# Expert outputs through DRAM rows for seven expert pairs instead of five, written by index, and one more weight buffer

## The chip, the cores and the metric

One core of a Trainium2 chip runs the whole kernel. The metric is the device time of one execution in microseconds (us): the median of the runs shown.

## The reference, cut to what matters

One decoder layer on 512 tokens of 1024 numbers: two attention branches, then a mixture of 32 experts, of which every token takes two, and a final RMSNorm. The change lies in the mixture:

```python
expert_id = g_sel[:, None] * EXPERTS_PER_GROUP + top_idx      # two experts of one group for each token
weight = p_group * jax.nn.softmax(top_vals, axis=-1)
...
def expert_block(args):
    xb, e = args
    return (jax.nn.silu(xb @ w_g[e]) * (xb @ w_u[e])) @ w_d[e]   # 1024 -> 256 -> 1024
...
out = jnp.zeros((T, D), h.dtype).at[slot_tok].add(ys * slot_w[:, None])
```

Every expert has three weight matrices of 1 MB in float32 (gate, up, down), 96 MB for all 32.

## The kernel before

The work runs in this order: RMSNorm and transposes; the projections and the attention of the first branch (MLA), then of the second (MoBA); the merge gates; the product with w_out, with the router's arithmetic between its matmuls; then the experts, two at a time, in 16 steps q = 0 to 15 (`experts`, L862); then the final norm.

**Slots.** Each expert has 64 slots, a pair fills 128 partitions: the first 64 are one expert's, the others the next one's. The 512 tokens take two experts each, so 1024 of the 2048 slots hold a token; in an empty slot the token number `xf` is 0 (tokens are counted from -1024, L663 and L1234), and its row index `xi` is 1024, outside the table. A path for experts with more than 64 tokens (`overflow`, L993) exists; in this execution it does nothing.

**One step.** TensorE multiplies the pair's rows `xT` with the gate weights (32 matmuls, L778), then with the up weights (32, L778); ScalarE and VectorE make the activation `a`; TensorE transposes it (L790) and multiplies with the down weights (16, L804). The rows of pair q + 2 are fetched by index from DRAM on the POOL queue (`gather_rows`, L731: rows `xg`, router weights `wg`) during step q, and transposed in step q + 1 (L755).

**Two ways for a pair's output to reach the tokens.** Pairs that are not in `VIA = (1, 3, 5, 7, 9)` are combined: the output is split into a high and a low part (L811, L812), a one-hot matrix `S` of slots by tokens is made (L817), and for each of 8 pieces (2 halves of the columns, 4 token tiles) two matmuls (L824, L825) bring the rows to their tokens and one VectorE addition (L826) adds them to `x2`. These 8 pieces are done in the next step or the next two: from step 1 to step 10 at most four in a step (L899), after that all eight. The five pairs in `VIA` write the output, 128 rows of 4 KB with the empty slots, to the DRAM table `yd` by one plain DMA of POOL (`down_out`, L843). In steps 10 to 13, two indirect DMAs of POOL a step (`take_slots`, L852) fetch for the 128 tokens of one tile the row of each choice, where that choice lies in a `VIA` pair; two VectorE additions (L914) add them in the step after.

**Weights.** SP's queue loads the weights of the experts, one DMA of 1 MB for each matrix (`load`, L686); each waits until the third last one has landed (L688), so at most three are in flight, and until its buffer is free. `new_w` (L677) deals out NH = 20 buffers of 8 KB a partition in a ring: buffer 0 has a place of its own, the others are spaces that the attention and the w_out stage leave. The output tile `y` has another space, 2 x 4 KB a partition (tag "yd", L846 and L855). The loads of a pair come as gate, gate, up, up, down, down.

**Order.** PE and POOL in the expert stage run in the order in which the code is written (L869); elsewhere a scheduler orders the instructions of a queue. Each queue runs in order: an instruction that waits holds up all behind it.

Of the kernel before, what the change touches and what calls it, by code (L numbers as in the profile page):

```python
# [10 lines left out]
F32 = mybir.dt.float32  # L11
# [3 lines left out]
I32 = mybir.dt.int32  # L15
# [6 lines left out]
P = 128  # L22
# [10 lines left out]
NH = 20  # L33
VIA = (1, 3, 5, 7, 9)


class Layer:
# [310 lines left out]
    def moba_qkv(self):  # L348
# [5 lines left out]
        self.V[1] = self.half("Vb", F32, (NT, 512))  # L354
        late = []

        def split_T(which, t, qr):
# [32 lines left out]
    def attention(self, br, pairs):  # L390
# [4 lines left out]
        for m in pairs:  # L395
# [30 lines left out]
            for i, k in ((i, k) for i in range(NT) for k in range(i + 1)):  # L426
                for h in range(2):
                    hh = 2 * m + h
                    E = Es[2 * i + h][2]
                    mm = nc.tensor.matmul(O[64 * h:64 * h + 64, i * P:(i + 1) * P], self.V[br][:, k, hh * 64:(hh + 1) * 64],  # L430
                                          E[:, k * P:(k + 1) * P], start=k == 0, stop=k == i)
                    if first is None:
                        first = mm
                        for c in PT[2:]:
                            self.after(mm, c)
# [198 lines left out]
    def route_setup(self):  # L634
# [8 lines left out]
        for g in range(4):  # L643
# [13 lines left out]
                          .to_broadcast([P, 32]))  # L657
        self.rc = c.tile([P, 33 + NT + NE], F32, name="rc")
        self.load_late(self.rc, io["rconst"])
        self.iota32 = self.rc[:, 0:32]  # L660
        self.slot = self.rc[:, 32:33]
        self.token = self.rc[:, 33:33 + NT]
        self.base = self.rc[:, 33 + NT:]  # L663
        self.tri = c.tile([P, 2, P], F16, name="tri")
# [12 lines left out]
    def new_w(self):  # L677
        i = self.nw % NH
        self.nw += 1
        if i == 0:  # L680
            return self.bl.tile([P, 2048], F32, name="w", tag="w", bufs=1)
# [146 lines left out]
    def slot_rows(self):  # L828
# [11 lines left out]
        self.yi = c.tile([P, NT, 2], I32, name="yi")  # L840
        nc.vector.tensor_tensor(self.yi, rows, far, ALU.add)

    def down_out(self, wd, aT, sw, q):  # L843

        nc = self.nc
        y = self.bl.tile([P, D], F32, name="y", tag="yd", bufs=2)  # L846
        for h in range(2):
            nc.scalar.mul(y[:, h * 512:h * 512 + 512], self.down_products(wd, aT, h), sw)
        i = VIA.index(q) * P
        nc.gpsimd.dma_start(self.yd[i:i + P], y)  # L850

    def take_slots(self, t, i):  # L852

        nc = self.nc
        y = self.bl.tile([P, D], F32, name="y", tag="yd", bufs=2)  # L855
        nc.gpsimd.memset(y, 0.0)
# [5 lines left out]
    def experts(self):  # L862
# [6 lines left out]
        with tc.manual_schedule(engines={mybir.EngineType.PE, mybir.EngineType.Pool}):  # L869
            xT, sw, xg = {0: self.xT0}, {}, {}  # L870
            S, y, todo, taken = None, None, [], []
            for q in range(NP):
# [11 lines left out]
                def between(j):  # L884
                    if q == 0 and j == 3:
                        self.tokens()
                        xg[1] = self.gather_rows(self.xi[:, 1:2], self.rows)
                    if q == 0 and j == 5:
                        sw[0] = self.take_weights()
# [7 lines left out]
                if q == 0:  # L897
                    next_rows()
                n = min(len(todo), 4) if VIA[0] <= q <= VIA[-1] + 1 else len(todo)  # L899
                some((n + 1) // 2 + (n > 4))  # L900
                aT = self.act_T(*a)
                if q:
                    sw[q] = [self.slot_weights(q, wg, nc.scalar.copy)[:, 0:1]]
                some(n // 2 - (n > 4))
                if 0 < q < NP - 1:
# [145 lines left out]
    def run(self):  # L1051
        tc, ctx = self.tc, self.ctx
        self.oT = [None, None]
        self.nw, self.loads, self.rf = 0, [], {}
        PS = dict(space=PSUM, reuse_waits="tile")
# [157 lines left out]
def shape_consts():  # L1213
# [15 lines left out]
    out["tri"] = tri  # L1229
    rc = np.zeros((P, 33 + NT + NE), np.float32)  # L1230
    rc[:, 0:32] = np.arange(32)
    rc[:, 32] = 1025 + np.arange(P) % 64
    rc[:, 33 + NT:] = [64 * (2 * VIA.index(i // 2) + i % 2) - 1025 if i // 2 in VIA else 1 << 20 for i in range(NE)]
    rc[:, 33:33 + NT] = np.arange(P)[:, None] + P * np.arange(NT)[None, :] - 1024  # L1234
    out["rconst"] = rc
    out["tm"] = np.broadcast_to(np.arange(T, dtype=np.float32) - 1024, (P, T)).copy()
# [31 lines left out]
```

## Time and profile before

| | |
|---|---|
| median of 3 runs | 682.37 us (682.04 to 683.69) |
| the profiled execution | 683.7 us |
| its span, first to last instruction | 681.9 us |
| mean granted TensorE clock | 0.989 of full speed |
| TensorE busy with matmuls | 661.3 us (97%) |
| VectorE, ScalarE, POOL busy | 376.1, 283.3, 83.3 us |
| moved by DMA | 152.06 MB, mean 223 GB/s |

The profiled execution is the slowest of the three; 1.8 us of it lie outside its span, and it is 1.3 us above the median. Matmuls are pipelined, so that a busy TensorE is one that has been given work, not one at its peak. Idle time of an engine that is not the bound costs nothing.

### The profile page before, as it was taken

The page shows a single profiled execution, that of the slowest core. Times are in us where ns is not written, and L with a number is a line of the kernel's source. Part 1 is how long each engine was busy: PE and PEld are TensorE (multiplying, and loading weights), DVE is VectorE, ACT ScalarE, POOL GpSimd, SP SyncE. Part 2 cuts the span into 40 slices and gives each one's busy share as a digit, 9 for nine tenths or more (in the row PEclk, how much of TensorE's full clock was granted, in tenths as well). Part 3 has the DMA queues.
Part 4 walks back from the last instruction along what each step waited for, and adds up shares of the span by engine and source line. Part 5 has one row for each costly group of instructions (what it writes and reads, how often), then busy time and mean ns, then how long its engine had stood idle before and what let it go on. Part 6 is the DMA issues. An engine that isn't in the chain of part 4 may idle for free.

```text
span 681.9 us, 11080 instructions
## 1 busy us (share of the span) xinstructions
PE 661.3 (97%) x4182; PEld 508.6 (75%) x4182; DVE 376.1 (55%) x944; ACT 283.3 (42%) x653; POOL 83.3 (12%) x127
## 2 busy tenths in 40 slices
PE   7999999999999999999999999999999999999991
PEld 7998887777788888888888899755666566666651
DVE  4624957877847983533568224643234332566654
ACT  4737545654639673433334153322222222222223
POOL 0604000000000000000000001212111111334303
PEclk8999999999999999999999999999999999999996
DMA  7733442101073026221398948799999999999953
GB/s 254 128 103 66 86 163 73 62 1 62 15 200 96 1 63 185 68 87 62 137 331 306 392 169 287 256 408 408 409 415 416 410 410 414 415 412 416 413 194 125
DMA packets 75656, 152.06 MB, mean 223 GB/s; under 512 B 31860, under 2 KB 54476, under 8 KB 63824
## 3 DMA queue, kind: packets, MB, share of 16 engines
q1 hardware_dynamic: 67616, 138.70, 55.9%
q0 software_dynamic: 4944, 8.35, 3.6%
q10 hardware_dynamic: 3040, 4.27, 2.4%
q8 instruction: 34, 0.56, 0.3%
q14 instruction: 22, 0.18, 0.1%
HBM read 149.57 MB, written 6.88 MB: 229 GB/s over the span
## 4 chain that ended last, share of the span: by engine, by line
PE 92%; DVE 4%; ACT 1%; DMA 1%; issue 1%; POOL 0%; SPq 0%; POOLq 0%; DVEq 0%
PE yp L804 8%; PE G L778 8%; PE U L778 8%; PE pacc L97 5%; PE pacc L96 5%; PE pacc L95 5%; PE pacc L451 4%; PE pacc L449 4%; PE pacc L450 4%; PE cp L824 3%; PE ptr L422 3%; PE cp L825 3%; PE S L404 3%; PE O L430 2%; PE pacc L493 2%; PE pacc L494 2%
## 5 line engine op out<-in xcount | busy, mean ns | idle before, releaser
L66 DVE SCALAR_TENSOR_TENSOR wlo<-wraw,ms,whi 128x256 fp32r<-128x256 f32 (+2 forms) x134 | 68.3, 551 | 31.1 <-ACT whi L65 30.9
L65 ACT ACTIVATE whi<-wraw,ms 128x256 fp32r<-128x256 f32 (+2 forms) x134 | 67.0, 560 | 42.1 <-PE pacc L450 19.8
L95 PE MATMUL pacc<-whi,hThi 128*128 128x352 f32 (+1 forms) x192 | 73.0, 380 | 0.0
L96 PE MATMUL pacc<-wlo,hThi 128*128 128x352 f32 (+1 forms) x192 | 70.4, 368 | 0.0
L97 PE MATMUL pacc<-whi,hTlo 128*128 128x352 f32 (+1 forms) x192 | 70.4, 366 | 0.0
L784 DVE SCALAR_TENSOR_TENSOR a<-U,wg,a 128x256 f32<-128x256 f32 x15 | 10.3, 686 | 101.8 <-issue 68.9
L804 PE MATMUL yp<-w,a 128*64 128x512 f32 x256 | 58.5, 598 | 0.5 <-ACT a L792 0.5
L778 PE MATMUL G<-w,xT 128*64 128x256 f32 x512 | 58.3, 380 | 0.0
L778 PE MATMUL U<-w,xT 128*64 128x256 f32 x512 | 58.2, 379 | 0.0
L778 PEld LDWEIGHTS G<-w,xT 128*64 128x64 f32 x512 | 36.5, 137 | 24.6 <-issue 4.9
L826 DVE TENSOR_TENSOR x<-x,cp 128x512 f32<-128x512 f32 x88 | 54.2, 682 | 0.8 <-PE cp L825 0.8
L778 PEld LDWEIGHTS U<-w,xT 128*64 128x64 f32 x512 | 36.7, 137 | 18.4
L449 PE MATMUL pacc<-hThi,whi 128*128 128x512 f32 x128 | 50.4, 393 | 0.0
L451 PE MATMUL pacc<-hThi,wlo 128*128 128x512 f32 x128 | 50.3, 393 | 0.0
L450 PE MATMUL pacc<-hTlo,whi 128*128 128x512 f32 x128 | 49.9, 390 | 0.0
L417 ACT ACTIVATE E<-E,mx 128x128 f32<-128x128 f32 (+3 forms) x64 | 35.6, 558 | 20.4 <-DVE mx L414 19.6
L1107 POOL TENSOR_SCALAR sq<-sq 128x1 f32<-128x1 f32 x4 | 0.9, 220 | 343.4 <-ACT junk L1104 343.4
L95 PEld LDWEIGHTS pacc<-whi,hThi 128*128 128x128 f32 x192 | 36.5, 190 | 4.9 <-issue 1.4
L96 PEld LDWEIGHTS pacc<-wlo,hThi 128*128 128x128 f32 x192 | 36.6, 191 | 4.2 <-issue 0.7
L804 PEld LDWEIGHTS yp<-w,a 128*64 128x64 f32 x256 | 17.0, 136 | 30.2 <-issue 27.8
L97 PEld LDWEIGHTS pacc<-whi,hTlo 128*128 128x128 f32 x192 | 36.4, 189 | 3.9 <-issue 0.2
L824 PE MATMUL cp<-yhl,S 128*128 128x512 f32 x88 | 37.6, 427 | 0.0
(232 smaller groups left out, 1338.8 us busy)
## 6 DMA issues: line engine op xcount, KB each, us to landing
w<-in_w_exp_gate_dram SPq DMA_DIRECT2D x32, 1024.0 KB
w<-in_w_exp_up_dram SPq DMA_DIRECT2D x32, 1024.0 KB
w<-in_w_exp_down_dram SPq DMA_DIRECT2D x30, 1024.0 KB
wraw<-in_w_in_dram SPq DMA_DIRECT2D x14, 1024.0 KB
wraw<-in_w_out_dram SPq DMA_DIRECT2D x4, 1024.0 KB
wraw<-in_w_in_dram SPq DMA_DIRECT2D x5, 704.0 KB
yd<-y POOLq DMA_DIRECT2D x5, 512.0 KB, 8.5
xs<-in_x_dram SPq DMA_DIRECT2D x4, 512.0 KB
```

The costliest lines, as they stand in the source:

```text
L65: nc.scalar.mul(hi[:, k], raw[:, k], g)
L66: nc.vector.scalar_tensor_tensor(lo[:, k], raw[:, k], g, hi[:, k].bitcast(F32), ALU.mult, ALU.subtract)
L95: nc.tensor.matmul(ps[t][:, :ncols], act_hi[kk // 4][:, kk % 4, ts], hi[:, k], start=kk == 0, stop=False)
L96: nc.tensor.matmul(ps[t][:, :ncols], act_hi[kk // 4][:, kk % 4, ts], lo[:, k], start=False, stop=False)
L97: nc.tensor.matmul(ps[t][:, :ncols], act_lo[kk // 4][:, kk % 4, ts], hi[:, k], start=False, stop=kk == ktot - 1)
L449: nc.tensor.matmul(ps, hi[:, k, ds], self.hT[0][k // 4][:, k % 4], start=k == 0, stop=False)
L450: nc.tensor.matmul(ps, hi[:, k, ds], self.hT[1][k // 4][:, k % 4], start=False, stop=False)
L451: nc.tensor.matmul(ps, lo[:, k, ds], self.hT[0][k // 4][:, k % 4], start=False, stop=k == KD - 1)
L778: nc.tensor.matmul(GU[i][es, 0:256], xT[:, j, es], gu[e][i][:, j * 256:(j + 1) * 256], start=j == 0, stop=j == KD - 1)
L804: nc.tensor.matmul(yp[es], aT[:, j, es], wd[e][:, j * D + half * 512:j * D + half * 512 + 512], start=j == 0, stop=j == 1)
L824: nc.tensor.matmul(cp, S[:, t * P:(t + 1) * P], y[0], start=True, stop=False)
L826: nc.vector.tensor_tensor(self.x2[t][:, hs], self.x2[t][:, hs], cp, ALU.add)
```

## The change

The pairs that go through DRAM become (1, 2, 4, 5, 7, 8, 9). Their rows are written by an indirect DMA whose index `yw` sends empty slots out of bounds, where nothing is written. So that every row of `yd` has been written once, two DMAs of SP copy 512 and 384 rows of `x` into it, after the first matmul of the first attention that multiplies with V (L430). The eight pieces of a combined pair are spread evenly over the steps up to the next combined pair: (3, 3, 2) over three steps, (2, 2, 2, 2) over four, eight in one step after pair 10 and later. The two halves of `y` become one tile of 8 KB a partition, `yy`, which first serves as a weight buffer for the very first load; the ring of 20 begins with the second. The router weights of pair 0 are taken (L888) after the eighth group of gate matmuls instead of the sixth.

```diff
--- before.py
+++ after.py
@@ -31,7 +31,7 @@
 NEG = -1e30
 NE = 32
 NH = 20
-VIA = (1, 3, 5, 7, 9)
+VIA = (1, 2, 4, 5, 7, 8, 9)
 
 
 class Layer:
@@ -353,6 +353,9 @@
         self.KB = [self.ktiles(n, F32R) for n in ("KBhi", "KBlo")]
         self.V[1] = self.half("Vb", F32, (NT, 512))
         late = []
+        for i in range(0, len(VIA) * P, T):
+            n = min(T, len(VIA) * P - i)
+            self.after(nc.sync.dma_start(self.yd[i:i + n], self.io["x"][0, 0:n, :]), self.first_pv)
 
         def split_T(which, t, qr):
             qf = qr.rearrange("p h c -> p (h c)")
@@ -431,6 +434,8 @@
                                           E[:, k * P:(k + 1) * P], start=k == 0, stop=k == i)
                     if first is None:
                         first = mm
+                        if (br, m) == (0, 0):
+                            self.first_pv = mm
                         for c in PT[2:]:
                             self.after(mm, c)
             self.evac_split(self.oT[br][0][:, m], self.oT[br][1][:, m], O)
@@ -655,12 +660,13 @@
         self.load_late(self.rb[:, 0:4], io["b_router_group"][0:1, :].to_broadcast([P, 4]))
         self.load_late(self.rb[:, 8:40], io["b_router_expert"].rearrange("o g e -> o (g e)")
                           .to_broadcast([P, 32]))
-        self.rc = c.tile([P, 33 + NT + NE], F32, name="rc")
+        self.rc = c.tile([P, 33 + NT + NE + len(VIA)], F32, name="rc")
         self.load_late(self.rc, io["rconst"])
         self.iota32 = self.rc[:, 0:32]
         self.slot = self.rc[:, 32:33]
         self.token = self.rc[:, 33:33 + NT]
-        self.base = self.rc[:, 33 + NT:]
+        self.base = self.rc[:, 33 + NT:33 + NT + NE]
+        self.own = self.rc[:, 33 + NT + NE:]
         self.tri = c.tile([P, 2, P], F16, name="tri")
         self.after(nc.gpsimd.dma_start(self.tri, io["tri"]), self.started)
         self.tm = c.tile([P, T], F16, name="tm")
@@ -675,8 +681,11 @@
 
 
     def new_w(self):
-        i = self.nw % NH
+        i = (self.nw - 1) % NH
         self.nw += 1
+        if self.nw == 1:
+            self.yy = self.bl.tile([P, 2048], F32, name="w", tag="yd", bufs=1)
+            return self.yy
         if i == 0:
             return self.bl.tile([P, 2048], F32, name="w", tag="w", bufs=1)
         pool, tag = {11: (self.wp, "wraw"), 12: (self.wp, "wraw"), 13: (self.wp, "whi"), 14: (self.wp, "wlo"),
@@ -839,20 +848,30 @@
         nc.vector.tensor_tensor(rows, rows, self.place, ALU.add)
         self.yi = c.tile([P, NT, 2], I32, name="yi")
         nc.vector.tensor_tensor(self.yi, rows, far, ALU.add)
+        free = c.tile([P, NE // 2], F32, name="free")
+        nc.vector.tensor_scalar(free, self.xf, -0.5, float(1 << 20), ALU.is_gt, ALU.mult)
+        self.yw = c.tile([P, len(VIA)], I32, name="yw")
+        for i, q in enumerate(VIA):
+            nc.vector.tensor_tensor(self.yw[:, i:i + 1], free[:, q:q + 1], self.own[:, i:i + 1], ALU.add)
+
+    def new_y(self):
+        self.ny += 1
+        return self.yy[:, self.ny % 2 * D:self.ny % 2 * D + D]
 
     def down_out(self, wd, aT, sw, q):
 
         nc = self.nc
-        y = self.bl.tile([P, D], F32, name="y", tag="yd", bufs=2)
+        y = self.new_y()
         for h in range(2):
             nc.scalar.mul(y[:, h * 512:h * 512 + 512], self.down_products(wd, aT, h), sw)
-        i = VIA.index(q) * P
-        nc.gpsimd.dma_start(self.yd[i:i + P], y)
+        i = VIA.index(q)
+        nc.gpsimd.indirect_dma_start(out=self.yd, out_offset=bass.IndirectOffsetOnAxis(ap=self.yw[:, i:i + 1], axis=0),
+                                     in_=y, in_offset=None, bounds_check=len(VIA) * P - 1, oob_is_err=False)
 
     def take_slots(self, t, i):
 
         nc = self.nc
-        y = self.bl.tile([P, D], F32, name="y", tag="yd", bufs=2)
+        y = self.new_y()
         nc.gpsimd.memset(y, 0.0)
         nc.gpsimd.indirect_dma_start(out=y, out_offset=None, in_=self.yd,
                                      in_offset=bass.IndirectOffsetOnAxis(ap=self.yi[:, t, i:i + 1], axis=0),
@@ -885,7 +904,7 @@
                     if q == 0 and j == 3:
                         self.tokens()
                         xg[1] = self.gather_rows(self.xi[:, 1:2], self.rows)
-                    if q == 0 and j == 5:
+                    if q == 0 and j == KD - 1:
                         sw[0] = self.take_weights()
                     if q == 0 and j == 9:
                         self.count_blocks()
@@ -896,12 +915,13 @@
                         self.gathered_T(xg[q + 1][0], xT[q + 1], g)
                 if q == 0:
                     next_rows()
-                n = min(len(todo), 4) if VIA[0] <= q <= VIA[-1] + 1 else len(todo)
-                some((n + 1) // 2 + (n > 4))
+                n = -(-len(todo) // next(d for d in range(1, NP) if q + d - 1 not in VIA))
+                first = n if n < 4 else (n + 1) // 2 + (n > 4)
+                some(first)
                 aT = self.act_T(*a)
                 if q:
                     sw[q] = [self.slot_weights(q, wg, nc.scalar.copy)[:, 0:1]]
-                some(n // 2 - (n > 4))
+                some(n - first)
                 if 0 < q < NP - 1:
                     next_rows()
                 if q + 1 < NP:
@@ -1051,7 +1071,7 @@
     def run(self):
         tc, ctx = self.tc, self.ctx
         self.oT = [None, None]
-        self.nw, self.loads, self.rf = 0, [], {}
+        self.nw, self.ny, self.loads, self.rf = 0, 0, [], {}
         PS = dict(space=PSUM, reuse_waits="tile")
         SB = dict(reuse_waits="tile")
         ctx.enter_context(tc.tile_pool(name="edge", bufs=1, side="right")).tile([P, 24], F32, name="pad")
@@ -1227,11 +1247,12 @@
     tri[:, 0] = np.arange(P)[:, None] <= np.arange(P)[None, :]
     tri[:, 0] += 1024.0 * np.eye(P)
     out["tri"] = tri
-    rc = np.zeros((P, 33 + NT + NE), np.float32)
+    rc = np.zeros((P, 33 + NT + NE + len(VIA)), np.float32)
     rc[:, 0:32] = np.arange(32)
     rc[:, 32] = 1025 + np.arange(P) % 64
-    rc[:, 33 + NT:] = [64 * (2 * VIA.index(i // 2) + i % 2) - 1025 if i // 2 in VIA else 1 << 20 for i in range(NE)]
+    rc[:, 33 + NT:33 + NT + NE] = [64 * (2 * VIA.index(i // 2) + i % 2) - 1025 if i // 2 in VIA else 1 << 20 for i in range(NE)]
     rc[:, 33:33 + NT] = np.arange(P)[:, None] + P * np.arange(NT)[None, :] - 1024
+    rc[:, 33 + NT + NE:] = np.arange(P)[:, None] + P * np.arange(len(VIA))[None, :]
     out["rconst"] = rc
     out["tm"] = np.broadcast_to(np.arange(T, dtype=np.float32) - 1024, (P, T)).copy()
     return out
```

## Rows read from the trace of the kernel before

**Rows 1.** The page: busy time of each engine, and the DMAs in 40 slices.

```profile
PE 661.3 (97%) x4182; PEld 508.6 (75%) x4182; DVE 376.1 (55%) x944; ACT 283.3 (42%) x653; POOL 83.3 (12%) x127
...
DMA  7733442101073026221398948799999999999953
```

**Rows 2.** Stretches: PE, PEld, DVE, ACT, POOL busy, clock, DMA share, GB/s.

```profile
435.00:440.00 5.00, 5.00 (x48) 3.46 (x50) 2.94 (x14) 2.19 (x5) 1.19 (x1) 1.00 0.21 63
440.00:445.00 5.00, 4.99 (x46) 3.13 (x42) 1.45 (x6) 1.26 (x3) 1.02 (x1) 1.00 0.93 321
...
460.00:640.00 180.00, 180.00 (x1280) 109.60 (x1277) 78.18 (x128) 43.77 (x99) 46.64 (x47) 1.00 1.01 412
```

**Rows 3.** Waits of SP's queue: for what, us in total, times, longest.

```profile
SPq L687 <- DMA w<-in_w_exp_gate_dram: 65.9, 26, 6.9
...
SPq L687 <- PE G L778: 9.4, 2, 9.1
```

**Rows 4.** The chain that ended last: starts of the gate matmuls, steps 9, 10, 12, 13.

```profile
558.44 3.45 PE G L778 x32
...
572.11 3.45 PE G L778 x32
...
601.41 3.45 PE G L778 x32
...
617.04 3.45 PE G L778 x32
```

**Rows 5.** Timeline of PE: gate and up matmuls of step 15.

```profile
648.14 3.62 PE L778 MATMUL G<-w,xT 128*64 128x256 f32 x32
651.59 3.62 PE L778 MATMUL U<-w,xT 128*64 128x256 f32 x32
```

**Rows 6.** Timeline of SP: loads of weights as they are issued.

```profile
255.72 0.37 SPq L687 DMA_DIRECT2D w<-in_w_exp_gate_dram  x1
...
439.88 1.14 SPq L687 DMA_DIRECT2D w<-in_w_exp_up_dram  x2
...
443.66 0.33 SPq L687 DMA_DIRECT2D w<-in_w_exp_down_dram  x1
...
449.13 0.33 SPq L687 DMA_DIRECT2D w<-in_w_exp_gate_dram  x1
...
617.98 0.33 SPq L687 DMA_DIRECT2D w<-in_w_exp_gate_dram  x1
...
634.81 0.33 SPq L687 DMA_DIRECT2D w<-in_w_exp_gate_dram  x1
...
651.20 0.54 SPq L687 DMA_DIRECT2D w<-in_w_exp_down_dram  x1
```

**Rows 7.** The page: the queue of POOL's DMAs: packets, MB, share of 16 engines.

```profile
q0 software_dynamic: 4944, 8.35, 3.6%
```

**Rows 8.** Tile yd (its write; landing of its DMAs), then tile x2d (landing).

```profile
L850 POOL DMA_DIRECT2D yd<-y x5: 578/578/592, 463.8 to 573.2; - x5
...
DMA to landing us min/median/max: 7.9/8.7/9.6
...
DMA to landing us min/median/max: 7.6/7.9/8.2
```

**Rows 9.** Timeline: first V matmul, a w_in load, the first reader of its data.

```profile
119.20 2.40 PE L430 MATMUL O<-E,Va 128*64 128x128 f32 x40
...
129.45 0.37 SPq L49 DMA_DIRECT2D wraw<-in_w_in_dram  x1
...
178.51 0.72 ACT L65 ACTIVATE whi<-wraw,ms 128x512 fp32r<-128x512 f32 x1 [1.84 <-PE pacc L97]
```

**Rows 10.** A small VectorE operation of slot_rows.

```profile
L838 DVE TENSOR_SCALAR far<-place x1: 164/164/164, 433.4 to 433.4; 128x8 f32<-128x8 f32 x1
```

**Rows 11.** Stretches at the start of the span, columns as in rows 2.

```profile
5.00:10.00 5.00, 2.81 (x17) 2.55 (x15) 3.11 (x6) 3.48 (x7) 0.00 (x0) 0.80 1.04 415
10.00:15.00 5.00, 5.00 (x34) 4.96 (x33) 2.83 (x5) 2.36 (x5) 0.00 (x0) 0.86 0.89 288
```

## The prediction

> **What bounds the kernel now.** I began with the page: TensorE is busy for 97% of the span, and in the last third the DMAs are busy too [rows 1]. Two resources seem full at once, so the page alone can't say which of them a saving has to relieve. The stretches answer the first half: from 460 to 640 us TensorE is busy in 180.00 of 180 us and the DMA share is 1.01 at 412 GB/s, while just before, at 435 to 440, the DMAs stand at 0.21 [rows 2]. The reader should see that in the expert stage neither has room, and that the DMAs had room shortly before it.
>
> The waits of SP's queue tell why: in the stage its loads wait for earlier loads to land (65.9 us behind gate loads alone), and once, 9.1 us long, for the gate matmuls of pair 0 to free a buffer [rows 3]. So the stream of weights has 20 loads in before TensorE starts on pair 0; then it stands until a buffer comes free at 439.88, and runs without a gap to its end.
>
> The chain that ended last runs through TensorE. A step with four pieces of combining takes 572.11 - 558.44 = 13.67 us, one with eight 617.04 - 601.41 = 15.63 us [rows 4]. A pair's weights take 634.81 - 617.98 = 16.83 us to arrive [rows 6]. So the weights come slower than TensorE works, and the lead that they had at 439.88 melts. How much is left at the end? A load may only be issued when the third last before it has landed, so the issue at 651.20 tells that the last up matrix of pair 15 has landed [rows 6]. TensorE starts on it at 651.59, right behind the gate matmuls [rows 5]. **The slack is 0.4 us.** TensorE and the weight stream reach the end of the kernel together; the stage has two bounds, and what one of them saves alone is worth 0.4 us.
>
> **The change, part by part.**
>
> *TensorE.* Two more pairs go through DRAM: 16 pieces fewer (72 instead of 88). Four pieces cost 15.63 - 13.67 = 1.96 us [rows 4], one 0.49, so TensorE is given 16 x 0.49 = 7.8 us less. By the slack, 0.4 us of it counts; the rest becomes waiting for weights, from about step 11 on, unless the weights come earlier too.
>
> *The 21st buffer.* The very first load takes the space of the outputs, which is free as early as the buffer that the first load has now (255.72 us, [rows 6]); all others move up one place in the ring, so before the stop at 439.88 there are 21 loads in, not 20. A load is 1.05 MB, at 412 GB/s 2.55 us [rows 2]: the most it can bring. But `yy` never comes back as a weight buffer. Of the four buffers that pair 0's gate and up matmuls free, only three take new loads. Today two loads go out at 439.88 and one at 443.66, with the next behind it [rows 6]: four loads of 2.55 us and the row gathers follow one another, from about 440.4 to 451.7. After the change one load goes out at 439.88, lasts to about 443, and the next two can only go out when the up matmuls end, at 443.66; they are through at about 449.8, and the following two can go out when pair 0's down matmuls end, at about 449.1 as now [rows 6]. The stream is then ahead by some 1.9 us; the rest of the 2.55 is lost in a pause near 443. I take **2.0**, ends 0 and 2.55. The Trainium skill, "DMA: Bandwidth & Descriptors", section "Where 436 GB/s comes from", holds that loads from HBM are limited to about 358 GB/s for a core; by that a load would be worth 2.9 us, as an estimate, and the sum 0.4 more. The trace does not agree, it shows 412 GB/s, and the measurement decides.
>
> *Bytes of the outputs.* Now 5 writes of 128 rows and gathers of the valid half of 5 x 128: 640 + 320 = 960 rows of 4 KB. Afterwards 7 x 64 written and 7 x 64 fetched: 896. That is 64 rows or 0.26 MB less. POOL's queue takes 3.6% of 681.9 us for 8.35 MB [rows 7], 2.9 us for one MB, so **0.7 us** of all DMA engines. That half of the slots is valid is the code's count (1024 of 2048); the queue's 8.35 MB fit it, as full gathers of 15 x 0.52 MB would alone nearly fill them. No indirect write is in the trace: its nearest rows are the plain write and the gather from the same table (7.9 to 9.6 us to landing) and the gather of `x2d` (7.6 to 8.2) [rows 8]. At the rate of a gather it costs as reckoned; if each of its rows took the time of two, 448 rows would cost 5.4 us more, the bad end; the good end is a write that costs the stream nothing at all, 1.8 MB or 5.4 us. I take the gather's rate, since a gather moves rows of the same size by the same kind of index.
>
> *The fill of `yd`.* Two copies on SP's queue wait for the first V matmul, at 119.20 us; behind them on SP stand w_in loads, the nearest at 129.45, whose data is first read at 178.51 [rows 9]. 3.7 MB take 8.9 us at 412 GB/s, and 36 us at a quarter of it; both fit into the 49 us. Nothing. Without that cover each us past it would stall the projections.
>
> *Small things at nothing.* Eight more VectorE operations of 0.16 us [rows 10] lie beside pair 0's matmuls, where VectorE is busy for 2.94 of 5 us [rows 2]; the router weights of pair 0 move by two groups of gate matmuls and are still early for the up product. POOL issues two more writes of 0.6 to 1 us; it is far from full (46.64 of 180 us [rows 2]). The additions of fetched rows (16 gathers' worth in steps 10 to 13, eight DMAs) stay as they are. Spreading (3, 3, 2) instead of 4 changes which step does the pieces, not their sum. `y` has two halves as before, so a pair waits for the output two before it, more than 25 us back, and landing takes 9.
>
> **The sum.** 0.4 + 2.0 + 0.7 = 3.1 us. The stream of weights brings pair 15's last up matrix 2.7 us earlier, and TensorE, 7.8 us ahead by then, starts on it at once. What comes behind (up matmuls, eight pieces, down, combine, norm) is unchanged. The profiled execution goes from 683.7 to 680.6, its span from 681.9 to 678.8; the median shown is 1.3 lower, so **679.3 us**. Late next are the weights: TensorE should wait for them by about 7.8 - 3.1 = 4.7 us, in pieces of 1 to 2 us in steps 11 to 15.
>
> **The rivals.**
>
> A. *The whole TensorE saving shows*: 682.4 - 7.8 = 674.6. For it speaks the chain, nearly all TensorE. Against it, the 0.4 us of slack and the DMA share of 1.01: the loads would have to come 5 us sooner than the bytes allow.
>
> B. *The extra buffer brings nothing*, because the pause near 443 eats it or the scheduler orders the early loads otherwise: 0.4 + 0.7 = 1.1, 681.3. For it speaks that a buffer drops out of the ring in exactly the place where the stream waits for buffers.
>
> C. *Slower, by POOL's queue.* The indirect write names no fixed rows, so each waits on POOL until the one before has landed, and behind it stands the gather of rows for a later pair. Consecutive pairs come some 13 us apart. With a landing of X us the gather goes out late from X = 21, and TensorE is late from X = 24.5, where its spare is used up: four neighbouring writes, each X - 24.5 us, less the 4.7 that TensorE can lose. It decides from about X = 26.5; at 30 us: 679.3 + 4 x 5.5 - 4.7 = 697. Against it: the nearest landings are 7.6 to 9.6 us [rows 8].
>
> D. *Slower, by TensorE's clock.* Where TensorE had work for only 2.81 of 5 us at the start, the granted clock was 0.80 in that stretch and 0.86 in the next: for about 3.4 us it stood at 1.2 instead of 2.4 GHz [rows 11], which costs 1.7 us of matmul time. New waits could bring this back in each of the steps 11 to 15, whose spare is 16.83 - 15.63 = 1.2 us: 5 x 0.5 = 2.5 us lost if it happens once a step, 11 us if twice; say 686. A step would still be busy for 93%, against 56% in that row. The Trainium skill, "TensorE: Matmul & The Clock Gate", section "HAM oscillation — how this bites in real kernels", describes such a loop, in which each wait for a DMA throws the array back to half its clock; no run here shows it yet.
>
> E. *Empty slots are written all the same*: 384 rows more than now, 1.57 MB or 4.6 us, less 2.4: 684.6. The gathers leave their empty rows out by the same means, so this is unlikely.
>
> **How the numbers follow.** My forecast has 0.62, A 0.09, B 0.17, C 0.04, D 0.05, E 0.03. A measurement of this kernel can tell 0.3%, about 2 us, from no change; the line is 680.3. Of the forecast's 0.62, some 0.55 lies below it (the buffer's end at 0 and the write's bad end lie above): with A, faster 0.64. Same: the other 0.07 and B, 0.24. Slower: C, D and E, 0.12. The range leaves out A and the slow cases, about 2 in 10: from 676.5 (a buffer at its full 2.55 and writes that are nearly free) to 682.5, just above B.
>
> **What would show it.** Right: 21 loads issued before the stop near 439, and a pause of the DMAs near 443; first waits of TensorE for weights from step 11 on, none longer than about 2 us; the up matmuls of step 15 starting 2.5 to 3.5 us earlier, within 0.5 us of the issue that marks the landing; the clock at 1.00 throughout; the indirect write landing in 8 to 10 us. Wrong: the stream of weights not ahead at step 15; TensorE waiting for rows or for `y` instead of weights; a load of w_in that is late behind the two copies; a DMA share under 0.95 in the stage, which would mean that something other than bytes holds up the loads.

## The result and the profile after

The changed kernel takes **686.34 us** (median of 9 runs, 684.73 to 690.35), the kernel before 682.37 (9 runs, 682.03 to 683.87): a ratio of 1.0059, with a 95% interval of 1.0043 to 1.0075. It is slower by about 4 us, where 3.1 us less had been forecast. The median of the kernel before lay between 682.31 and 683.73 in the later sets of runs, so kernels are compared below by their ratios to it; a ratio is known to 0.0013 to 0.0019 either way (95%), about 1 us.

The page of the kernel after, the lines that answer to [rows 1] and [rows 7]:

```profile
PE 661.6 (97%) x4150; PEld 503.9 (74%) x4150; DVE 362.5 (53%) x930; ACT 283.0 (41%) x653; POOL 87.3 (13%) x129
...
DMA  8724432701172027311397957779999999999953
...
q0 software_dynamic: 5232, 7.98, 3.3%
...
L454 PE MATMUL pacc<-hThi,whi 128*128 128x512 f32 x128 | 51.0, 398 | 0.0
L456 PE MATMUL pacc<-hThi,wlo 128*128 128x512 f32 x128 | 50.9, 398 | 0.0
```

TensorE runs 32 matmuls fewer (the 16 pieces) and is busy for as long as before. The two groups at the end belong to a stage that the change doesn't touch, the gate projections of the dense part. On the page of the kernel before they are the lines

```profile
L449 PE MATMUL pacc<-hThi,whi 128*128 128x512 f32 x128 | 50.4, 393 | 0.0
...
L451 PE MATMUL pacc<-hThi,wlo 128*128 128x512 f32 x128 | 50.3, 393 | 0.0
```

Five ns more on each matmul, in code that is the same: that is the first thing to explain. Stretches of the kernel after, with the columns of [rows 2]:

```profile
256.00:326.00 70.00, 70.00 (x302) 56.31 (x301) 26.26 (x56) 25.28 (x55) 0.00 (x0) 1.00 0.36 112
440.00:445.00 5.00, 5.00 (x52) 3.28 (x50) 2.54 (x19) 1.07 (x3) 2.19 (x2) 1.00 0.52 97
447.00:449.00 2.00, 0.00 (x0) 0.00 (x0) 0.65 (x1) 0.00 (x0) 0.00 (x0) 1.00 0.72 194
449.00:451.00 2.00, 1.94 (x9) 1.94 (x10) 0.00 (x0) 0.62 (x2) 0.00 (x0) 0.53 1.01 422
451.00:453.00 2.00, 1.54 (x7) 0.50 (x7) 1.02 (x2) 0.37 (x1) 1.39 (x2) 0.62 1.00 418
453.00:455.00 2.00, 2.00 (x12) 0.70 (x10) 0.09 (x1) 0.69 (x1) 0.60 (x1) 1.00 0.53 201
460.00:640.00 180.00, 179.26 (x1286) 108.70 (x1284) 67.64 (x111) 45.16 (x105) 51.33 (x49) 1.00 1.01 416
```

and one stretch of the kernel before:

```profile
256.00:326.00 70.00, 70.00 (x310) 57.95 (x309) 26.62 (x56) 25.59 (x56) 0.00 (x0) 1.00 0.32 98
```

In the dense part, at a clock of 1.00 and with TensorE never idle, 302 matmuls start in 70 us where 310 did. And in step 0 of the experts TensorE does nothing from 447 to 449, after which its granted clock is 0.53 and 0.62 in two stretches of 2 us: for most of them it stood at 1.2 instead of 2.4 GHz. Its timeline shows where this sits, first after:

```profile
438.13 1.95 PE L787 MATMUL G<-w,xT 128*64 128x256 f32 x16
...
441.82 1.08 PE L619 MATMUL ptr<-W,hot 128*128 128x33 f32 x8
...
449.06 1.97 PE L764 MATMUL ptr<-ident,xg 128*128 128x128 f32 x8 [2.23 <-DMA xg<-x2d,xi]
...
455.69 3.62 PE L787 MATMUL G<-w,xT 128*64 128x256 f32 x32
...
653.19 0.59 PE L787 MATMUL U<-w,xT 128*64 128x256 f32 x2
```

then before:

```profile
434.93 1.95 PE L778 MATMUL G<-w,xT 128*64 128x256 f32 x16
...
438.77 1.08 PE L778 MATMUL G<-w,xT 128*64 128x256 f32 x8
...
443.57 1.16 PE L755 MATMUL ptr<-ident,xg 128*128 128x128 f32 x8
...
448.94 3.62 PE L778 MATMUL G<-w,xT 128*64 128x256 f32 x32
```

Four numbers add up to the whole difference of the spans, 684.6 - 681.9 = 2.7 us:
- **The front**: step 0 starts at 438.13 instead of 434.93, 3.20 us late.
- **Step 0**: 455.69 - 438.13 = 17.56 us instead of 448.94 - 434.93 = 14.01, 3.55 us more. The transposes of pair 1's rows start 10.93 us into the step instead of 8.64 (2.29 more, the wait of 2.23 for the gather); from there to the next step it takes 6.63 us instead of 5.37 (1.26 more, the clock).
- **Steps 1 to 14**, up to the up matmuls of step 15: 653.19 - 455.69 = 197.50 us instead of 651.59 - 448.94 = 202.65 [rows 5], 5.15 us less. Here the gain that was meant must show, but only half of it is that gain: with the large tiles at their old addresses (first experiment below) the same stretch takes 652.69 - 452.54 = 200.15 us, 2.5 less than before. The other half goes with the addresses: from the 27th load to the mark of the last up matrix (651.20 in [rows 6]) the loads take 194.7 us in the kernel after and 196.6 with the old addresses, one profile each; why is open.
- **Behind that** 31.4 us instead of 30.3, 1.1 more, of which 0.9 lies ahead of the down matmuls of step 15.

The profiled run of before was itself 1.3 us over its median (its 683.69 against 682.37), that of after was not (686.37): 2.7 and 1.3 make the 4.0 of the medians.

So the 3.20 us of the front are not the whole price of what happens there, for the profile of before starts worse. Its granted clock is 0.80 and 0.86 in the stretches from 5 to 15 us, in which 17 and 34 matmuls start [rows 11]; in the kernel after it is

```profile
5.00:10.00 5.00, 3.43 (x26) 3.21 (x25) 3.48 (x7) 3.91 (x8) 0.00 (x0) 1.00 1.04 415
10.00:15.00 5.00, 5.00 (x38) 4.85 (x36) 3.61 (x7) 2.58 (x5) 0.08 (x1) 1.00 0.89 292
```

The executions differ in this start, whatever the kernel: at the old addresses step 0 starts anywhere from 433.28 to 435.20 us in the profiles below. Without it, from the start of the 101st matmul (at 19 to 21 us) to step 0, the kernel before takes 413.9 us and the kernel after 418.9: what happens there costs 5.0 us.

Why does the gather come late? SP's loads around step 0, each shown as it is issued:

```profile
430.03 0.38 SPq L696 DMA_DIRECT2D w<-in_w_exp_up_dram  x1
...
441.93 0.33 SPq L696 DMA_DIRECT2D w<-in_w_exp_up_dram  x1
446.86 0.33 SPq L696 DMA_DIRECT2D w<-in_w_exp_down_dram  x1
...
455.88 0.80 SPq L696 DMA_DIRECT2D w<-in_w_exp_gate_dram  x2
...
653.99 0.54 SPq L696 DMA_DIRECT2D w<-in_w_exp_down_dram  x1
```

and POOL's gather of pair 1's rows, first after, then before:

```profile
441.39 1.18 POOL L745 DMA_INDIRECT xg<-x2d,xi  x1 [7.37 <-DVE free L852]
...
438.19 1.19 POOL L736 DMA_INDIRECT xg<-x2d,xi  x1 [7.37 <-DVE xi L599]
```

The load at 430.03 is the 21st, as forecast. The 22nd goes out at 441.93, while POOL is still issuing the gather (to 442.57). The packets of that gather (from the trace's DMA packets) move from 446.3 to 448.7 us only, behind the megabyte. In the kernel before the gather was issued by 439.38, half a microsecond ahead of the loads at 439.88 [rows 6], and its packets moved from 440.1 to 441.8. Measured from the start of the step the gather stands where it stood (3.26 us in, both times); it is the load that comes earlier, 3.80 us in instead of 4.95. It waits for a gate buffer, and with the router weights' matmuls (L619) moved behind the last group of gate matmuls, the gate matmuls end about 1 us sooner: their last group, at 438.77 before, is done 4.9 us into the step, and after it is done when the router weights' matmuls start at 441.82, 3.7 us in. SP's waits name that place, and the wait for pair 0's down matmuls behind it:

```profile
SPq L696 <- PE yp L813: 8.5, 5, 7.5
SPq L696 <- PE ptr L619: 8.2, 1, 8.2
```

So the theory, before any experiment: a gain as forecast, and over it two losses that no term of the sum had. **First**, the new small constants (28 bytes more in `rc`, 64 in `free`, 28 in `yw` on each partition, 120 together) move all the large tiles behind them by 128 bytes, and the dense part's matmuls of 512 columns run slower there. **Second**, the moved router weights let a weight load overtake the gather. The rivals: the matmuls are slowed by something else that the change brings early (the fill of `yd`, the extra load at 255 us), and the late gather comes from the 21st buffer.

### The profile page after: what moved, and what is told of

It is laid out like the page before. It is cut to its first block, busy times and chain, and to the rows that moved or that the text cites. A ratio compares the mean times of both kernels' runs of the same rounds, so it can differ in the third digit from the quotient of the medians.

```text
span 684.6 us, 11007 instructions
## 1 busy us (share of the span) xinstructions
PE 661.6 (97%) x4150; PEld 503.9 (74%) x4150; DVE 362.5 (53%) x930; ACT 283.0 (41%) x653; POOL 87.3 (13%) x129
## 3 DMA queue, kind: packets, MB, share of 16 engines
q0 software_dynamic: 5232, 7.98, 3.3%
## 4 chain that ended last, share of the span: by engine, by line
PE 86%; DMA 8%; DVE 2%; ACT 1%; issue 1%; SPq 0%; POOL 0%; POOLq 0%; DVEq 0%; ACTq 0%
PE yp L813 7%; PE U L787 7%; PE G L787 6%; PE pacc L97 6%; PE pacc L96 5%; PE pacc L95 5%; PE pacc L456 4%; PE pacc L454 4%; PE pacc L455 4%; DMA w<-in_w_exp_up_dram 3%; PE ptr L425 3%; PE S L407 3%; DMA w<-in_w_exp_gate_dram 3%; PE O L433 2%; PE pacc L498 2%; PE pacc L500 2%
## 5 line engine op out<-in xcount | busy, mean ns | idle before, releaser
L787 PE MATMUL U<-w,xT 128*64 128x256 f32 x512 | 60.2, 380 | 0.9 <-DMA w<-in_w_exp_up_dram 0.5
L787 PEld LDWEIGHTS U<-w,xT 128*64 128x64 f32 x512 | 38.1, 137 | 19.7 <-DMA w<-in_w_exp_up_dram 2.3
L835 DVE TENSOR_TENSOR x<-x,cp 128x512 f32<-128x512 f32 x72 | 44.6, 683 | 0.6 <-PE cp L834 0.6
L801 ACT COPY a<-G 128x256 f32<-128x256 f32 x16 | 6.0, 372 | 73.4 <-PE G L799 56.9
```

The source lines that it names most:

```text
L787: nc.tensor.matmul(GU[i][es, 0:256], xT[:, j, es], gu[e][i][:, j * 256:(j + 1) * 256], start=j == 0, stop=j == KD - 1)
L835: nc.vector.tensor_tensor(self.x2[t][:, hs], self.x2[t][:, hs], cp, ALU.add)
```

## The experiments

In the step starts below, step 0 means the first gate matmul of pair 0, "U15" the first up matmul of step 15 and "the mark" the load whose issue tells that the last up matrix has landed.

**Old addresses alone.** The kernel after with 128 bytes on each partition taken back, 64 of old padding and the 64 of `free`, which goes into a scratch tile; so the large tiles lie where they lay before:

```diff
-        c.tile([P, 16], F32, name="pad")
...
-        free = c.tile([P, NE // 2], F32, name="free")
+        free = junk[:, 0:NE // 2]
```

> The changed kernel with its big tiles back at the addresses of the kernel before (128 bytes lower). Theory (the new small constants moved every large tile by 128 bytes, and float32r matmuls with 512 columns then take 229 to 238 ns instead of 227): the matmuls of the gate stage are at 227 ns again, the gate matmuls of step 0 start about 3.2 us earlier (near 435 us of the span instead of 438.1), and the median falls by about 3.2 us from 686.3 to 683.1. Rival (the two copies into DRAM, the order of the scheduler, or the rotation of the large buffers slow the front): the gate stage stays at 229 to 238 ns, step 0 starts near 438, the median stays within 0.5 us of 686.3.

Measured: 683.21 us, ratio 0.9993 (0.998 to 1.0006), against 1.0059 for the kernel after: 0.0066 of 683, 4.5 us back. The stretch in the dense part is that of before again:

```profile
256.00:326.00 70.00, 70.00 (x311) 57.94 (x310) 26.62 (x56) 25.49 (x56) 0.00 (x0) 1.00 0.36 113
```

Step 0 starts at 434.80, 413.9 us after the 101st matmul as before the change. It still takes 17.74 us, with a wait of 2.01 for the rows:

```profile
445.52 1.16 PE L763 MATMUL ptr<-ident,xg 128*128 128x128 f32 x8 [2.01 <-DMA xg<-x2d,xi]
```

The fill of `yd` and the early load are both in this kernel, so they are not what slows the matmuls.

**The shift alone, in the kernel before**, by 128 bytes, and later by 512 and by 64:

```diff
-        c.tile([P, 16], F32, name="pad")
+        c.tile([P, 48], F32, name="pad")
```

(144 floats for 512 bytes, 32 for 64.)

> The kernel before with 128 bytes more of padding among its constants, nothing else. Theory (addresses alone): its 512-column matmuls of the gate stage go from 227 to about 233 ns on average, step 0 starts 3 to 5 us later than 434.9, and the median rises from 682.4 by about 3.2 us to 685.6. Rival (addresses don't matter, something else in the change slows the front): within 0.5 us of 682.4.

> The kernel before with 512 bytes more of padding among its constants. If the rate of the 512-column float32r matmuls depends on addresses with a period of 512 bytes or less that 128 does not divide evenly, the gate stage stays at 227 ns a matmul and the time within 1 us of the kernel before; if every shift costs, it goes to about 232 ns and 3.5 us more.

> The kernel before with 64 bytes more of padding. If the cost grows with the distance, the gate stage lies between 227 and 232 ns a matmul; if any address other than the tuned one costs, at 232 ns or more, with 3 us or more on the time; if half of 128 is as good as none, 227 ns.

By 128 bytes: 686.89 us, ratio 1.005 (1.0032 to 1.0068); nothing of the change is in this kernel, and it loses 3.4 us (2.2 to 4.6 by the interval). Its step 0 starts at 437.90. By 512 and 64 bytes, one run each: 683.32 and 684.22 us, step 0 at 434.68 and 435.55. Both times lie within those of the kernel before in the same set (681.68 to 685.45) and settle nothing; the traces do. From the 101st matmul to step 0 the nine profiles with the old addresses take 413.9 to 414.0 us, 512 bytes further on it is 413.9, 64 bytes 416.2, and 128 bytes 418.2 to 418.9 (three kernels): nothing, 2.3 and 4.3 to 5.0 us. The same stretch at 128 bytes:

```profile
256.00:326.00 70.00, 70.00 (x303) 56.74 (x302) 26.58 (x56) 25.27 (x55) 0.00 (x0) 1.00 0.31 97
```

at 512:

```profile
256.00:326.00 70.00, 70.00 (x311) 57.96 (x310) 26.62 (x56) 25.33 (x56) 0.00 (x0) 1.00 0.31 97
```

and at 64:

```profile
256.00:326.00 70.00, 70.00 (x308) 57.43 (x307) 26.20 (x56) 25.25 (x55) 0.00 (x0) 1.00 0.30 97
```

The median time from one matmul's start to the next, for the three kinds of gate matmuls (worked out from the trace's starts):

```
                       hThi,whi  hTlo,whi  hThi,wlo   (ns)
before                   226       227       227
before + 512 bytes       226       227       227
before +  64 bytes       229       232       226
before + 128 bytes       232       232       232
after (+ 128 bytes)      235       234       234
after, old addresses     226       227       227
```

At 64 bytes the three kinds differ among themselves, so none of the three forms expected fits as it stands, though the 2.3 us are about half of the price at 128. So it is where the operands lie that counts, and not that something else runs beside. Which relation of which addresses makes it, these runs don't tell.

**Router weights back, alone.** The kernel after with the old place:

```diff
-                    if q == 0 and j == KD - 1:
+                    if q == 0 and j == 5:
```

> The changed kernel with the router weights of pair 0 taken after the sixth group of gate matmuls again, as before the change; nothing else. Theory (with the later place the gate matmuls end 1 us earlier, so that the next weight load goes out about 0.6 us ahead of the gather of pair 1's rows, which then lands behind it): the gather is issued ahead of that load, its rows are there when the up matmuls end, step 0 (gate start to the next gate start) falls from 17.6 us to about 14.2, the loads behind it go out some 3 us earlier, and the median falls by 2.5 to 3.5 us to about 683.3. Rival (the gather is late because there is a 21st load in the DMAs, or for another reason): step 0 stays near 17.6 us and the median within 0.7 us of 686.3.

Measured: 684.83 us, ratio 1.0021 (1.0007 to 1.0036), 0.0038 or 2.6 us better than the kernel after. (In the profile step 0 starts 1.13 us later, as the first 15 us run slower: 18 and 35 matmuls start in the two stretches shown above, not 26 and 38.) Step 0 takes its 14.01 us again, with no wait for rows, though all else of the change is there, the 21st buffer too:

```profile
439.26 1.95 PE L787 MATMUL G<-w,xT 128*64 128x256 f32 x16
...
447.90 1.15 PE L764 MATMUL ptr<-ident,xg 128*128 128x128 f32 x8
...
453.27 2.98 PE L787 MATMUL G<-w,xT 128*64 128x256 f32 x26
```

**The late place in the kernel before** (the same line the other way round):

> The kernel before with the router weights of pair 0 taken after the eighth group of gate matmuls instead of the sixth; nothing else. Theory (that place alone lets a weight load overtake the gather of pair 1's rows): step 0 grows from 14.0 us to about 17, the loads that wait for its down matmuls go out 3 us later, and, since weights and TensorE reach the end together in this kernel, the median rises by 2 to 3.5 us, to 684.5 to 686. Rival (the place is harmless by itself and needs the 21st load): within 0.6 us of the kernel before.

Measured: 688.59 us, ratio 1.0067 (1.0048 to 1.0085). That is more than I had expected, and the trace offers a reason: without the 21st buffer in the ring two loads, not one, wait for the gate buffers, and both overtake the gather issued at 438.40. Its packets move from 443.4 to 448.1. SP:

```profile
438.93 0.98 SPq L687 DMA_DIRECT2D w<-in_w_exp_up_dram  x2
```

and TensorE:

```profile
435.14 1.95 PE L778 MATMUL G<-w,xT 128*64 128x256 f32 x16
...
448.15 1.63 PE L755 MATMUL ptr<-ident,xg 128*128 128x128 f32 x8 [4.30 <-DMA xg<-x2d,xi]
...
454.84 3.62 PE L778 MATMUL G<-w,xT 128*64 128x256 f32 x32
```

Step 0 is 5.69 us longer: 4.37 to the transposes and 1.32 behind them, the clock again. U15 starts 222.29 us after step 0, before 216.66, so nearly all of it reaches the up matmuls of step 15: in this kernel, bound by TensorE, a stall of TensorE has no cover.

**The late place kept, the load held back.** The kernel after at the old addresses, whose 22nd load may only go out when the gather has landed:

```diff
+        if len(self.loads) == 21:
+            self.after(d, self.gathered)
```

> The changed kernel at the old addresses, router weights at their late place, and the first load that waits for a gate buffer (the 22nd) held until the gather of pair 1's rows has landed. Theory (the late place hurts only because that load gets ahead of the gather): the rows land in time, step 0 falls from 17.7 us (late place, not held) to about 14.3, and the median lies 2 to 3 us under that of the late place not held, within 1 us of the kernel with the early place (0.996 of the kernel before). Rival (the late place hurts by its own work on TensorE and VectorE): step 0 stays near 17.7 us and the ratio near 0.999 to 1.000.

Measured: 681.8 us, ratio 0.9977 (0.9963 to 0.9991). Step 0 takes 14.00 us:

```profile
434.89 1.95 PE L790 MATMUL G<-w,xT 128*64 128x256 f32 x16
...
443.53 1.16 PE L767 MATMUL ptr<-ident,xg 128*128 128x128 f32 x8
...
448.89 3.62 PE L790 MATMUL G<-w,xT 128*64 128x256 f32 x32
```

In step 0 the late place does no harm of its own; the overtaking does. The load is held back, to 441.75, and U15 still comes sooner: 214.50 us behind step 0 instead of 217.89. In the times it shows less. By the ratios (0.9977 against 0.9993) the hold brings 1.1 us, where 2 to 3 were expected, and the two intervals overlap. The runs without the hold lie far apart (680.97 to 684.81), and the profiled one was the longest of them; whether the overtaking is as long in every run isn't known.

**Both repairs at once** (the edits of the first and the third experiment):

> Both edits: large tiles at the old addresses and the router weights of pair 0 at their old place. If both theories hold and add, the median is 686.3 - 3.2 - 3.0 = 680.1, and what is left is the change as it was meant: 1.5 to 3.5 us faster than the kernel before, with TensorE waiting for weights from about step 11 on. If only one holds, about 683; if neither, 686.

Measured: 681.29 us, ratio **0.9962** (0.9944 to 0.998), 2.6 us faster than before (1.4 to 3.8), which is what was forecast of the whole change but for 0.5. Step 0 starts at 434.90 and takes 14.00 us. Its TensorE in step 15, with the answer to [rows 5]:

```profile
648.91 3.84 PE L786 MATMUL U<-w,xT 128*64 128x256 f32 x32
```

the mark, which stood at 651.20 [rows 6]:

```profile
649.06 0.54 SPq L695 DMA_DIRECT2D w<-in_w_exp_down_dram  x1
```

TensorE's waits for weights, and the clock in the stretch that holds the longest:

```profile
PE U L786 <- DMA w<-in_w_exp_up_dram: 2.7, 3, 1.4
```

```profile
600.00:640.00 40.00, 37.51 (x243) 23.65 (x240) 23.80 (x37) 7.24 (x17) 13.42 (x12) 1.00 1.02 411
```

U15 starts 2.68 us earlier than before (forecast 2.7), within 0.2 us of the mark. Up to step 11 TensorE is 7.3 us ahead of its steps in the kernel before; steps 12 to 14 then take 16.52, 17.70 and 17.34 us instead of 15.63, and give 4.67 of it back to the weights (forecast 4.7, in pieces of 1 to 2). The trace books only 2.7 of that as waits, since the ends of matmuls are modelled.

**What the parts bring.** From the kernel with both repairs on, one part is taken away each time. Without the 21st buffer (outputs in a tile of their own, first load in the ring):

```diff
-        i = (self.nw - 1) % NH
+        i = self.nw % NH
...
-        if self.nw == 1:
-            self.yy = self.bl.tile([P, 2048], F32, name="w", tag="yd", bufs=1)
-            return self.yy
...
+        self.yy = self.bl.tile([P, 2048], F32, name="y", tag="yd", bufs=1)
```

> The kernel with both repairs, but the space of the outputs is not a weight buffer: 20 loads before the stop instead of 21, and no buffer drops out. Theory (the 21st buffer is worth about 2 us of the weight stream): the last up matrix lands 2 us later, and the ratio to the kernel before is 0.998 to 0.999 (1.1 us faster) instead of 0.996. Rival (the pause that the lost buffer brings eats it): the ratio stays at 0.996 within 0.5 us.

Measured: 681.97 us, ratio 0.9989 (0.9973 to 1.0005). Against 0.9962 the buffer brings 1.8 us by the ratios; in the traces U15 follows step 0 by 648.39 - 433.37 = 215.02 us instead of 214.01, so 1.0. The two intervals just overlap, so the size is uncertain.

With plain writes of all 128 rows in place of the indexed ones:

```diff
-        nc.gpsimd.indirect_dma_start(out=self.yd, out_offset=bass.IndirectOffsetOnAxis(ap=self.yw[:, i:i + 1], axis=0),
-                                     in_=y, in_offset=None, bounds_check=len(VIA) * P - 1, oob_is_err=False)
+        nc.gpsimd.dma_start(self.yd[i * P:(i + 1) * P], y)
```

> The kernel with both repairs, but the seven outputs are written by plain DMAs with all 128 rows, the empty slots too. Theory (rows cost the weight stream by their bytes): 7 x 128 - 430 = about 460 rows or 1.9 MB more, 4.5 to 5.5 us of the stream, and TensorE's spare does not help: ratio about 1.003 to 1.005 (684 to 686). Rival (a plain write of full rows is as cheap as an indirect one of half as many): ratio stays at 0.996.

Measured: 684.56 us, ratio 1.0015 (1.0002 to 1.0028), 3.6 us behind the kernel with both repairs. POOL's queue moves 9.89 MB instead of 7.98; the mark comes 217.46 us after step 0 instead of 214.16, so 3.3 us for 1.91 MB, 1.7 us/MB (1.9 by the ratios; 4.5 to 5.5 us had been expected). This run has the longest wait for weights of all, 2.27 us, and there the clock falls:

```profile
586.10 4.99 PE L786 MATMUL U<-w,xT 128*64 128x256 f32 x30 [2.27 <-DMA w<-in_w_exp_up_dram]
```

```profile
585.00:595.00 10.00, 8.90 (x48) 5.96 (x49) 3.81 (x7) 0.75 (x3) 0.00 (x0) 0.83 1.01 411
```

The 30 matmuls take 4.99 us instead of 3.67. The DMA share stays at 1.01, and TensorE had time to lose here, as it was waiting for the weights.

With six pairs through DRAM, and with the five of before:

```diff
-VIA = (1, 2, 4, 5, 7, 8, 9)
+VIA = (1, 2, 4, 5, 7, 9)
```

(and `VIA = (1, 3, 5, 7, 9)`.)

> The kernel with both repairs and six pairs through DRAM, (1, 2, 4, 5, 7, 9), instead of seven. Theory (with seven pairs the weights are the bound and TensorE has about 4 us to spare): TensorE is given 3.9 us more, which its spare covers, and the stream of weights loses some 126 rows or 0.52 MB, 1 to 1.5 us: ratio 0.995 to 0.996, as fast as seven pairs or up to 1 us faster. Rival (TensorE sets the end also with seven pairs): 3 us slower than seven pairs, ratio about 1.000.

> The kernel with both repairs and the five pairs of the kernel before, (1, 3, 5, 7, 9); the indirect writes and the 21st buffer stay. Theory (two bounds that meet): the stream of weights is ahead by about 4 us, but TensorE has as much to do as before the change, so that nearly nothing is gained, ratio 0.998 to 1.000. Rival (the stream of weights alone is the bound): fewer bytes make it faster still, ratio under 0.994.

Measured: six pairs 681.28 us, ratio 0.9974 (0.9959 to 0.9989); five pairs 681.89, ratio 0.9991 (0.9978 to 1.0004). With six, TensorE waits for up weights once, for 0.2 us, and U15 comes 213.68 us after step 0: six and seven can't be told apart, neither by these times nor by the ratios (0.9974 and 0.9962; 0.995 to 0.996 had been expected). With five pairs, the first gate matmul, U15 and the mark:

```profile
433.28 1.95 PE L786 MATMUL G<-w,xT 128*64 128x256 f32 x16
...
649.93 3.62 PE L786 MATMUL U<-w,xT 128*64 128x256 f32 x32
```

```profile
647.02 1.82 SPq L695 DMA_DIRECT2D w<-in_w_exp_down_dram  x2
```

The weights are there 2.9 us before TensorE gets to them, and U15 follows step 0 by 216.65 us, before 216.66. All that the buffer and the rows give the stream is worth nothing in the stage while TensorE has its old work. That is the bound of TensorE alone; the kernel with both repairs shows the bound of the stream alone, and the forecast's two bounds are both there.

## Why the prediction was wrong

The forecast was 679.3 us, the range 676.5 to 682.5; 686.34 came out, on the side that had 0.12, though by none of the three ways that made up the 0.12.

*The mechanism that was costed is there.* The slack, the meeting of two bounds at step 15, the 21 loads, the pause (DMA share 0.52 from 440 to 445, 0.93 before [rows 2]), the waits of TensorE from step 12 on (forecast 11): with both side effects gone they stand as described. The gain is 2.6 us by the ratio and 2.65 in the stage, forecast 3.1. That it comes so near is in part luck, as errors cancel: by the traces the buffer was put too high (2.0; 1.0, though the ratios with 1.8 would allow it), the slack and the rows too low (1.1; 216.66 - 215.02 = 1.64). A row's price of 2.9 us/MB, taken from the share of POOL's queue, was too high (1.7).

*The step that failed first is one that the sum doesn't have.* "The change part by part" costs the new instructions, the new loads and the moved ones, and says nothing of where tiles lie. `rc`, `free` and `yw` were read as "small things" by the work done on them (0.16 us an operation [rows 10]), and that was right; what was left out is that their 120 bytes a partition move the large tiles. That costs the 3.4 us that the kernel before loses when it is shifted and nothing else is done to it, and 4.5 in the kernel after by the ratios; by the traces 4.3 to 5.0 us ahead of step 0. No row read for the prediction could have shown the price, as it takes a second layout. The diff did show that the layout changes.

*The second is "the router weights of pair 0 move by two groups of gate matmuls and are still early for the up product."* They are. What was left out is what the move lets go: the gate matmuls end sooner, and on SP a load stands waiting for just that. The rows for it were in the prediction's hands: the stop of 9.1 us for the gate matmuls [rows 3], the load at 439.88 [rows 6]; what it took of the gathers is their bytes in that stretch, not their place: that POOL issues the one for pair 1 only half a microsecond ahead of the load. It cost 2.3 us of waiting and 1.3 of clock in the profiled run, 2.6 by the ratios.

The two together: 1.0059 - 0.9962 = 0.0097, 6.6 us; taken away one by one, 4.5 and 2.6.

*The steps costed at nothing that were nothing*: the fill of `yd` holds SP for 11.0 us (a wait for the first V matmul) and the next w_in load goes out at 127.94, before 129.45 [rows 9]; step 0 of the kernel with both repairs starts at 434.90, as before, with the eight more VectorE operations ahead of it.

*The rivals.* A fell: the kernel with both repairs is nowhere near 674.6. B fell, if not by much: without the buffer the stage is 1.0 us longer in the trace and the time 1.8 by the ratios. C didn't come: the DMAs of `yd` land in 7.5 to 7.8 us (7.9 to 9.6 before [rows 8]). E fell: POOL's queue moved 7.98 MB, less than before, and 1.91 more when all slots are written. D is half right, at another place. "The clock at 1.00 throughout" is wrong: after a wait of 2.2 us for rows, of 4.3 in the kernel before with the late place, and of 2.27 for weights with plain writes, the clock fell to about half, each time at a loss of some 1.3 us; with the old addresses alone, after a wait of 2.01, it was 7.02 us instead of 5.37 from the transposes on, 1.65 (there the transposes still ran at full clock, and it fell some 2 us later). After the waits of up to 1.4 us in steps 12 to 14 it stayed at 1.00. The Trainium skill, "TensorE: Matmul & The Clock Gate", section "HAM oscillation — how this bites in real kernels", describes how a wait for a DMA throws the array back to half its clock; the runs agree in that, but none shows the loop that it draws: by 453 to 455 us the clock is at 1.00 again, and from 460 to 640 it is 1.00.

## What to carry to other kernels

When a change adds even a few bytes of constants, look at the spacing of matmuls in stages that it doesn't touch, and give back or pad the bytes before judging the change. Measure that spacing over a stretch that leaves out the kernel's first microseconds, where executions of one kernel differ. When an instruction is moved, ask not only whether its own result is in time, but whose buffer comes free sooner now, which queue stands waiting for it, and which small transfer that lets itself be overtaken. Where two resources reach the end together, relieve both, and only until they meet: here six pairs did what seven did, and five pairs with the faster stream did next to nothing.

## What was not expected of the hardware

- Matmuls of 512 columns in fp32r start every 227 ns or every 229 to 241, by where their tiles lie: 128 bytes further on cost 2 to 3% of the gate matmuls and 4.3 to 5.0 us of the time to step 0, 512 nothing, 64 half of it (2.3 us) and not for every operand. Why is open.
- The weight loads of the expert stage ran faster at the addresses where those matmuls ran slower. From the 27th load to the mark, one profile each: 194.7 us in the kernel after (196.6 with the old addresses), 195.3 with the router weights back (196.5 with the old addresses too), 194.7 in the kernel before shifted by 128 bytes (196.4 unshifted). Why is open.
- The rows of a gather whose issue ended 0.5 us before a load of 1 MB went out had moved 2.4 us later; where the load went out 0.6 us before that issue ended, they moved 3.7 to 6.2 us after it, behind the load (3.9 to 8.5 where two loads went ahead).
- A TensorE that had waited for 2.0 to 4.3 us fell to about half its clock, at once (0.53 over the next 2 us in the kernel after) or some 2 us later (with the old addresses alone), and lost another 1.3 to 1.7 us; after waits of up to 1.4 us it kept 1.00.
